# Second feed-forward matrix, block 0: one column block multiplied by halves of the rows, one with alternating PSUM banks

## The chip, the cores and the metric

The kernel runs on one core of a Trainium2 chip. The time is that of the device, in microseconds, for one execution of the whole program on that core. The engines that matter are TensorE (PE in the profile; its weight loads are listed apart as PEld), VectorE (DVE), ScalarE (ACT), GpSimd (POOL) and the queue of SyncE (SP), which issues the loads of weights. TensorE writes its products to PSUM banks of 128 partitions by 512 float32 values.

## What is computed

One encoder layer over 256 positions of width 2048: attention with a window, then a feed-forward part, each with scale, shift and gate from a conditioning vector and followed by a layer norm. The change is in the feed-forward part:

```python
def sq_relu_mlp(h, w1, b1, w2, b2):
    u = jnp.square(jax.nn.relu(h @ w1 + b1))
    return u @ w2 + b2
...
y = sq_relu_mlp(hff, mlp_w1[i], mlp_b1[i], mlp_w2[i], mlp_b2[i])
x = layer_norm(DEEPNORM_ALPHA * x + (1.0 + g_f[:, None, :]) * y, ln_mlp_g[i], ln_mlp_b[i])
```

Here `h` is 256 x 2048, `w1` is 2048 x 8192 and `w2` is 8192 x 2048, all float32.

## The kernel before

**Products.** TensorE is fed float32r, a shorter float32. So that little is lost, every operand is split into a high part (a rounded copy, made on ScalarE, line 277 for weights) and a low part (the difference, made on VectorE, line 230), and one product of 128 x 128 by 128 x 512 is three matmuls into the same bank: high by high, high by low, low by high (`mm3`, lines 544, 545 and 546). Each matmul loads its stationary operand, the activations, anew; the weights are the moving operand.

**Blocks.** The 8192 hidden columns go in four blocks of 2048 (`BLK = 4`). Block 0 first makes its hidden values `us` with lines 1032 to 1034, and then multiplies them with its 2048 rows of the second matrix. Only in block 0 is this done for all four column blocks `c` of 512 outputs in the plain way by `ff_out` and `ff_mm`; blocks 1 to 3 mix the first matrix with half of the second one (`ff_mixed`, whose first matmuls are those of line 1060) and use `ff_out` for the column blocks 2 and 3 alone.

**One column block.** `ff_out` takes two banks, one for each half `t` of the 256 positions. It goes through 16 slices `k` of 128 hidden columns: four loads of weights (`kg`), in each two pairs of slices (`k2`), in each pair first the six matmuls of `t` = 0 and then the six of `t` = 1. That is 16 x 2 x 3 = 96 matmuls. After each pair `S.done()` gives a pair of weight buffers back, and more weights are prepared. After the column block two adds on VectorE (line 1179) bring the two banks and the bias row to SBUF, one add for each `t`; with them the banks come free.

**Banks.** The pool `psa` has five banks for all of these products (`bufs=5`); two more pools hold the remaining three banks. A tile taken from the pool gets a bank that nothing uses any more; the first matmul into it waits until the last reader of the tile before is through.

**The order of work.** Each engine runs its instructions in a fixed order, which is set when the program is built: by the order in the source, except where an instruction that comes later in the source is ready sooner. `Stream` (`S`) keeps the weights in order: it loads 128 x 2048 slices on the queue of SyncE, makes high and low parts in five buffers each, and between them gives VectorE the steps of the second gate (`m_gf`, `Mod.step`, line 378), two multiply-adds of 128 x 1024 for each slice of the gate's matrix. During block 0 a number of these slices are spread among the weights by the list `gf_fill`. The adds of line 1179 stand in the same queue of VectorE as those steps and the low parts.

Elsewhere the kernel has products that use only 64 of the 128 rows of the array: the scores of the attention (line 733), in plain float32, where two heads lie on the partitions 0 to 63 and 64 to 127 and write to two banks in turn. Every such product of the source is two instructions of 64 x 128 by 64 x 256 in the trace.

Of the kernel before, what the change touches and what calls it, by code (L numbers as in the profile page):

```python
# [11 lines left out]
F32 = mybir.dt.float32  # L12
# [8 lines left out]
S = 256  # L21
NT = S // 128
# [26 lines left out]
def hybrid_kernel(ctx: ExitStack, tc: tile.TileContext, a, out: bass.AP):  # L49
    nc = tc.nc  # L50
# [7 lines left out]
    psa = ctx.enter_context(tc.tile_pool(name="psa", bufs=5, space=PSUM))  # L58
# [9 lines left out]
    def g4b(dt=F32):  # L68
        if not more:
            early.close()  # L70
            more.append(ctx.enter_context(tc.tile_pool(name="gen2", bufs=2 * MORE)))
        return more[0].tile([128, 1024], dt, tag="g4b", name="g4b")

    def g4(dt=F32):
        return gen.tile([128, 1024], dt, tag="g4", name="g4")
# [93 lines left out]
    def bias_all(src, b):  # L169

        for h in range(2):
            nc.gpsimd.dma_start(b[h], src[:, h * 1024:h * 1024 + 1024].partition_broadcast(128))
        return lambda c: b[c // 2][:, (c % 2) * 512:(c % 2) * 512 + 512]
# [139 lines left out]
    S = Stream()  # L313
# [155 lines left out]
    for g in range(2, G):  # L469
        n = len(ORDER[g])  # L470
# [69 lines left out]
    def part(tiles, t, c):  # L540
        return tiles[c][:, t * 512:t * 512 + 512]

    def mm3(ps, xh, xl, wh, wl, start, stop):
        nc.tensor.matmul(ps, xh, wh, start=start, stop=False)  # L544
        nc.tensor.matmul(ps, xh, wl, start=False, stop=False)  # L545
        S.prev = nc.tensor.matmul(ps, xl, wh, start=False, stop=stop).ins  # L546
# [62 lines left out]
    def qkv(g, ch):  # L609

        _, k0, nk = m_mix[g]
        hh, hl = held[g]
        wh, wl = S.main()
        per = 4 // nk
        for ci in range(per):
            p = ch * per + ci
            c = CORD[p]
            go_on, held_back = c in half, ((g, ch), p) in CARRY
            pss = half.pop(c, None) or banks()
            for k2 in range(0, nk, 2):  # L620
                for t in range(NT):
                    for k in (k2, k2 + 1):
                        s = slice(k * 256 + t * 128, k * 256 + t * 128 + 128)
                        mm3(pss[t], hh[:, s], hl[:, s], wh(ci * nk + k), wl(ci * nk + k),
                            k == 0 and not go_on, k == nk - 1 and not held_back)
                S.done()
                if per == 1 and k2 == 0:
                    yield
            if held_back:
                half[c] = pss  # L630
            else:
                evict(c, pss)
            if per == 2 and ci == 0:
                yield
# [36 lines left out]
    for x, (g, c) in enumerate(qk_order):  # L671
        at = ORDER[g].index(c)
        mid = []
# [156 lines left out]
    def project(j, c):  # L830
        wh, wl = S.main()
        oh, ol = oT[j]
        pss = [psa.tile([128, 512], F32, name="pa") for _ in range(NT)]
        last = j == 3 and c == 3
        for t, rs in [(0, range(4)), (1, range(4))] if last else [(t, (r, r + 1)) for r in (0, 2) for t in range(NT)]:
            for r in rs:
                s = slice(t * 512 + r * 128, t * 512 + r * 128 + 128)
                mm3(pss[t], oh[:, s], ol[:, s], wh(r), wl(r), r == 0, r == 3)
            if t == 1 or last:
                S.done(not last)  # L840
            if last:
                add_gated(pss[t], t, c, g1, st)
                sc.append(norm_scalars(st[t]))
                normed(0, t)
            if t == 1 and rs[0] == 0:
                yield
        for t, ps in enumerate(pss):
            if j == 0:
                nc.vector.tensor_add(part(ys, t, c), ps, bo(c))
            elif j < 3:  # L850
                y = part(ys, t, c)
                nc.vector.tensor_add(y, y, ps)
                if j == 2:
                    z = part(xs, t, c)
                    nc.vector.tensor_mul(y, y, g1(c))
                    nc.vector.scalar_tensor_tensor(z, z, ALPHA, y, op0=OP.mult, op1=OP.add)
            elif not last:
                add_gated(ps, t, c, g1, st)
# [11 lines left out]
    def mids(n):  # L870
        out = []
        if 0 < n <= 16:
            out.append(lambda: probs_T(n - 1))
        if n < 16:
            out.append(lambda: normalise(n))
        return out
# [3 lines left out]
    for n in range(21):  # L880
# [10 lines left out]
        if n + 1 < len(LATE):  # L891
            w = qkv(*LATE[n + 1])
        else:
            if n == 5:
                ys, bo = [g4b() for _ in range(4)], bias_all(a["bo"], [g4b(), g4b()])
            w = project((n - 5) // 4, (n - 5) % 4)
        mid = mids(n)
# [116 lines left out]
    us = []  # L1014
    opened = {}
    for n, (kg, fq) in enumerate(W1A):
# [3 lines left out]
        wh, wl = S.main()  # L1020
        for fp in range(2):
            if kg % 2 == 0:
                opened[fq, fp] = psa.tile([128, 512], F32, name="pa")
            ps = opened[fq, fp]
            for fi in range(2):
                o = ps[:, fi * 256:fi * 256 + 256]
                for k in range(4):
                    w = (fp * 2 + fi) * 4 + k
# [10 lines left out]
            elif kg == 3:  # L1039
                nc.vector.tensor_add(av, av, ps)  # L1040
                u = g4(F32R)
# [67 lines left out]
    def gather(pm):  # L1109

        y = [part(ys, t, c) for t in range(NT) for c in range(2)]
        w = sml.tile([128, 512], F32, name="w", tag="t2", bufs=4)

        def add(d, *ops):
            return lambda: nc.vector.tensor_add(d, *ops)

        return [add(y[0], y[0], pm[2]), lambda: nc.scalar.copy(w, pm[6]), add(y[1], y[1], pm[3]),
                add(y[2], y[2], pm[4]), add(y[0], y[0], pm[1]), add(w, w, pm[1]), add(y[1], y[1], w),
                add(y[1], y[1], pm[5]), add(y[3], y[3], pm[5]), add(w, w, pm[7]), add(y[2], y[2], w),
                add(y[3], y[3], w)]  # L1120

    def ff_mm(ps, us, kg, t, w, start, stop, ks=range(4)):
        wh, wl = w
        for k in ks:
            n = 4 * kg + k
            s = slice((n % 2) * 256 + t * 128, (n % 2) * 256 + t * 128 + 128)
            u = us[n // 2]
            mm3(ps, u[:, :512][:, s], u[:, 512:][:, s], wh(k), wl(k), start and k == 0, stop and k == 3)

    def ff_out(blk, us, c, mid=()):  # L1130
        mid = list(mid)
        pss = [psa.tile([128, 512], F32, name="pa") for _ in range(NT)]
        for kg in range(4):
            w = S.main()
            for k2 in (0, 2):
                for t in range(NT):
                    ff_mm(pss[t], us, kg, t, w, kg == 0, kg == 3, (k2, k2 + 1))
                S.done()
                for f in mid[:2]:
                    f()  # L1140
                del mid[:2]
        return pss

    ys = [g4b() for _ in range(4)]
# [3 lines left out]
    def rescale(c):  # L1148
        gb = [sml.tile([128, 512], F32, name="gb", tag="t2", bufs=4) for _ in range(2)]
        for n in range(2):  # L1150
            nc.gpsimd.dma_start(gb[n], a["lnrow"][n:n + 1, c * 512:c * 512 + 512].partition_broadcast(128))
        for t in range(NT):
            z = part(xs, t, c)
            nc.vector.scalar_tensor_tensor(z, z, ALPHA, gb[0], op0=OP.mult, op1=OP.mult)
            nc.vector.scalar_tensor_tensor(z, gb[1], ALPHA, z, op0=OP.mult, op1=OP.add)

    def base(c, ts=range(NT)):
        for t in ts:
            y, z = part(ys, t, c), part(xs, t, c)
            nc.vector.tensor_mul(y, y, g2(c))  # L1160
            nc.vector.tensor_add(z, z, y)

    def row_bias(c):
        b = sml.tile([128, 512], F32, name="bf", tag="t2", bufs=4)
        nc.gpsimd.dma_start(b, a["b2"][:, c * 512:c * 512 + 512].partition_broadcast(128))
        return b

    for blk in range(BLK - 1):
        if blk:
            us, pm = ff_mixed(blk)  # L1170
        for c in (2, 3) if blk else range(4):
            mid = gather(pm) if blk and c == 2 else []
            for f in mid[:2]:
                f()
            if blk == 0:
                bf = row_bias(c)
            for t, ps in enumerate(ff_out(blk, us, c, mid[2:])):
                if blk == 0:
                    nc.vector.tensor_add(part(ys, t, c), ps, bf)
                else:  # L1180
                    nc.vector.tensor_add(part(ys, t, c), part(ys, t, c), ps)
            if blk:
                rescale(2 * blk + c - 4)
        if blk == 0:
            S.reserve = 2

    blk = BLK - 1
    g2 = gate(m_gf)
    us, pm = ff_mixed(blk, [lambda c=c, t=t: base(c, (t,)) for c in (2, 3) for t in range(NT)])
# [5 lines left out]
    mid = gather(pm)  # L1195
    for f in mid[:2]:
        f()
    pss = ff_out(blk, us, 2, mid[2:])
    for c in range(2):
        base(c)  # L1200
# [7 lines left out]
    for t in range(NT):  # L1208
        ps = psa.tile([128, 512], F32, name="pa")
# [108 lines left out]
```

## Time and profile before

| | |
|---|---|
| median of the runs | 1080.25 us (2 runs, 1079.69 and 1080.81) |
| the profiled execution | 1080.82 us, of which the span from the first to the last instruction is 1079.0 us |
| mean granted TensorE clock | 0.995 of full speed |
| DMA over the span | 292.70 MB, mean 271 GB/s |

"Busy" is the time in which at least one instruction of the engine runs. The ends of matmuls are modelled, and neighbours overlap in the trace: a matmul of 128 x 512 is listed with 390 ns, but the next one starts about 227 ns after it. What such a matmul costs is therefore read from start to start. In the lists of instructions in order of time the columns are start, duration (both in us), engine, line, operation, tiles and shapes, and in brackets the idle time before it with what ended it. In the tables by stretch the columns are the stretch, its length, and for each engine the busy time and the number of instructions that started, then the granted clock, the share of the DMA engines and GB/s.

### The profile page before, as it was taken

To read this page: it belongs to the slowest core of one execution; us is meant where nothing else is said; L and a number is where in the kernel's file an instruction comes from. 1 tells how busy PE (TensorE), PEld (TensorE's weight loads), DVE (VectorE), ACT (ScalarE), POOL (GpSimd) and SP (SyncE) were. 2 spreads that over 40 slices of the span, in tenths; PEclk is the share of its full clock that TensorE was granted. 3 is DMA by queue.
4 is the path that set the end of the run, shared out by engine and by line. 5 is a ranking of instruction groups with operands and counts; after the bars stand their busy time and mean duration, and the time that the engine had idled before them with its cause. 6 is when DMAs were issued, how large, how long until landed. Compare 5 with 4: busy or idle time off the path is not lost.

```text
span 1079.0 us, 15651 instructions
## 1 busy us (share of the span) xinstructions
PE 1049.8 (97%) x6018; PEld 847.9 (79%) x6018; DVE 926.3 (86%) x1371; ACT 611.4 (57%) x977; POOL 31.0 (3%) x56
## 2 busy tenths in 40 slices
PE   8889999999999999999999999999999999999995
PEld 6557677666667799988888888888888888888884
DVE  5598699988889898988679889969988887998997
ACT  5333347776773636644357677347767536776740
POOL 1000000001000000000000000000000001000001
PEclk9999999999999999999999999999999999999998
DMA  9999997779966798689725644954464684455632
GB/s 384 425 426 426 426 419 268 283 281 378 405 251 234 305 356 314 257 335 405 271 97 196 233 176 153 375 195 176 176 234 174 266 319 148 176 205 220 244 161 78
DMA packets 43371, 292.70 MB, mean 271 GB/s; under 512 B 5136, under 2 KB 5264, under 8 KB 9504
## 3 DMA queue, kind: packets, MB, share of 16 engines
q1 hardware_dynamic: 39312, 279.85, 66.7%
q0 software_dynamic: 3232, 10.50, 3.0%
q10 hardware_dynamic: 752, 1.35, 0.3%
q8 instruction: 47, 0.77, 0.3%
q14 instruction: 28, 0.23, 0.1%
HBM read 289.57 MB, written 2.11 MB: 270 GB/s over the span
## 4 chain that ended last, share of the span: by engine, by line
PE 85%; DMA 9%; DVE 4%; ACT 1%; issue 0%; SPq 0%; DVEq 0%; ACTq 0%
PE pa L1060 17%; PE pa L544 13%; PE pa L546 13%; PE pa L545 13%; PE pa L1062 8%; DMA raw<-in_wqkv 4%; PE pa L1033 3%; PE pa L1034 3%; PE pa L1032 3%; DMA raw<-in_modm 3%; PE pm L340 2%; DMA raw<-in_modf 2%; PE pa L733 1%; PE pa L789 1%; DVE wl L230 1%; DVE g L378 1%
## 5 line engine op out<-in xcount | busy, mean ns | idle before, releaser
L277 ACT CAST wh<-raw 128x1024 fp32r<-128x1024 f32 (+1 forms) x332 | 335.5, 1020 | 302.3 <-PE pa L546 136.2
L230 DVE TENSOR_TENSOR wl<-raw,wh 128x1024 fp32r<-128x1024 f32 (+1 forms) x332 | 388.5, 1183 | 79.8 <-ACT wh L277 74.6
L544 PE MATMUL pa<-wh,g 128*128 128x512 f32 x648 | 258.0, 399 | 4.4 <-ACT g L581 2.1
L546 PE MATMUL pa<-wh,g 128*128 128x512 f32 x648 | 252.2, 392 | 3.0 <-DVE g L567 2.4
L545 PE MATMUL pa<-wl,g 128*128 128x512 f32 x648 | 254.0, 392 | 0.0
L1060 PE MATMUL pa<-g,wh 128*128 128x512 f32 x768 | 193.4, 394 | 0.0
L1060 PEld LDWEIGHTS pa<-g,wh 128*128 128x128 f32 x768 | 139.8, 188 | 31.6 <-DVE rl L990 4.1
L544 PEld LDWEIGHTS pa<-wh,g 128*128 128x128 f32 x648 | 121.6, 188 | 39.3 <-issue 6.8
L546 PEld LDWEIGHTS pa<-wh,g 128*128 128x128 f32 x648 | 121.6, 188 | 33.1 <-DVE g L567 4.7
L545 PEld LDWEIGHTS pa<-wl,g 128*128 128x128 f32 x648 | 121.8, 188 | 25.9 <-issue 2.4
L1062 PEld LDWEIGHTS pa<-g,wl 128*128 128x128 f32 x768 | 104.8, 190 | 7.5
L1062 PE MATMUL pa<-g,wl 128*128 128x256 f32 x768 | 107.1, 283 | 0.0
L378 DVE SCALAR_TENSOR_TENSOR g<-raw,cact,g 128x1024 f32<-128x1024 f32 x65 | 82.6, 1278 | 1.5 <-DMA raw<-in_modf 1.3
L1033 PE MATMUL pa<-g,wh 128*128 128x256 f32 x256 | 72.7, 285 | 0.4 <-DVE g L961 0.4
L1032 PE MATMUL pa<-g,wh 128*128 128x256 f32 x256 | 72.6, 285 | 0.0
L1034 PE MATMUL pa<-g,wl 128*128 128x256 f32 x256 | 72.5, 284 | 0.0
L230 DVE TENSOR_TENSOR raw<-raw 128x1024 fp32r<-128x1024 f32 x48 | 58.7, 1223 | 8.5 <-ACT raw L277 6.6
L277 ACT CAST raw<-raw 128x1024 fp32r<-128x1024 f32 x48 | 50.6, 1054 | 12.0 <-PE pm L546 10.7
L340 PE MATMUL pm<-raw,cact 128*32 128x256 f32 (+2 forms) x768 | 47.3, 375 | 5.6 <-DMA raw<-in_modm 4.5
L1033 PEld LDWEIGHTS pa<-g,wh 128*128 128x128 f32 x256 | 49.1, 192 | 1.3 <-DVE g L961 0.8
L1032 PEld LDWEIGHTS pa<-g,wh 128*128 128x128 f32 x256 | 49.0, 192 | 0.4 <-ACT g L953 0.4
L1034 PEld LDWEIGHTS pa<-g,wl 128*128 128x128 f32 x256 | 49.1, 192 | 0.0
(220 smaller groups left out, 1210.0 us busy)
## 6 DMA issues: line engine op xcount, KB each, us to landing
raw<-in_w1b SPq DMA_DIRECT2D x48, 1024.0 KB, 5.6
raw<-in_w SPq DMA_DIRECT2D x40, 1024.0 KB, 8.4
raw<-in_modm SPq DMA_DIRECT2D x32, 1024.0 KB, 16.0
raw<-in_modf SPq DMA_DIRECT2D x32, 1024.0 KB, 8.8
raw<-in_wqkv SPq DMA_DIRECT2D x24, 1024.0 KB, 11.8
raw<-in_w2s SPq DMA_DIRECT2D x24, 1024.0 KB, 4.8
raw<-in_modgm SPq DMA_DIRECT2D x16, 1024.0 KB, 8.4
raw<-in_wo SPq DMA_DIRECT2D x16, 1024.0 KB, 7.6
```

Of the source, the lines that this page charges most:

```text
L230: self.pinned(nc.vector.tensor_sub(l[:, :w], r, f32(self.hs[n])[:, :w]))
L277: self.pinned(nc.scalar.copy(h[:, :s.shape[-1]], s))
L340: i = nc.tensor.matmul(self.ps[32 * j:32 * j + 32, :w], lhsT[j] if type(lhsT) is list else lhsT, rhs[j], start=self.first, stop=stop)
L378: nc.vector.scalar_tensor_tensor(p[:, :e], s, cact[:, kt:kt + 1], p[:, :e], op0=OP.mult, op1=OP.add)
L544: nc.tensor.matmul(ps, xh, wh, start=start, stop=False)
L545: nc.tensor.matmul(ps, xh, wl, start=False, stop=False)
L546: S.prev = nc.tensor.matmul(ps, xl, wh, start=False, stop=stop).ins
L1032: nc.tensor.matmul(o, wh(w, 128), hh, start=new, stop=False)
L1033: nc.tensor.matmul(o, wh(w, 128), hl, start=False, stop=False)
L1034: nc.tensor.matmul(o, wl(w, 128), hh, start=False, stop=end)
L1060: nc.tensor.matmul(ps, wh(k, 128), ff_in(k), start=k == 0, stop=False)
L1062: nc.tensor.matmul(ps[:, :256], wl(k, 128), ff_in(k)[:, :256], start=False, stop=k == NK - 1)
```

## The change

The second and the third column block of block 0 are done in other ways; the first and the fourth stay as they are.

For the second one (`c` = 1), `ff_out` takes four banks, two for each `t`. Every matmul over 128 rows becomes two over 64 rows each, `halves`: rows 0 to 63 into one bank, rows 64 to 127 into the other, in turn. The column block has 192 matmuls of 64 x 128 by 64 x 512 in place of 96 of 128 x 128 by 128 x 512. Each `t` then has two adds on VectorE, the first with the bias row and the first bank, the second with the second bank: four adds in place of two.

For the third one (`c` = 2), `ff_turns` does the same 96 matmuls in another order: for each slice and each of its three products, first `t` = 0 and then `t` = 1, so that two matmuls in a row never have the same bank or the same stationary operand.

```diff
+    def halves(ps, xh, xl, wh, wl, start, stop):
+        for n, (x, w) in enumerate(((xh, wh), (xh, wl), (xl, wh))):
+            for r in range(2):
+                p = slice(64 * r, 64 * r + 64)
+                S.prev = nc.tensor.matmul(ps[r], x[p], w[p], start=start and n == 0, stop=stop and n == 2).ins
+
+    def ff_turns(pss, us, kg, w, ks):
+        wh, wl = w
+        for k in ks:
+            n = 4 * kg + k
+            u = us[n // 2]
+            for m, (x, y) in enumerate(((0, wh), (0, wl), (512, wh))):
+                for t in range(NT):
+                    s = slice(x + (n % 2) * 256 + t * 128, x + (n % 2) * 256 + t * 128 + 128)
+                    nc.tensor.matmul(pss[t], u[:, s], y(k), start=n + m == 0, stop=n == 15 and m == 2)
...
-            mm3(ps, u[:, :512][:, s], u[:, 512:][:, s], wh(k), wl(k), start and k == 0, stop and k == 3)
+            (halves if split else mm3)(ps, u[:, :512][:, s], u[:, 512:][:, s], wh(k), wl(k),
+                                       start and k == 0, stop and k == 3)
...
-        pss = [psa.tile([128, 512], F32, name="pa") for _ in range(NT)]
+        pss = [[psa.tile([128, 512], F32, name="pa") for _ in range(2)] if split else
+               psa.tile([128, 512], F32, name="pa") for _ in range(NT)]
...
-                for t in range(NT):
-                    ff_mm(pss[t], us, kg, t, w, kg == 0, kg == 3, (k2, k2 + 1))
+                if blk == 0 and c == 2:
+                    ff_turns(pss, us, kg, w, (k2, k2 + 1))
+                else:
+                    for t in range(NT):
+                        ff_mm(pss[t], us, kg, t, w, kg == 0, kg == 3, (k2, k2 + 1), split)
...
-            for t, ps in enumerate(ff_out(blk, us, c, mid[2:])):
-                if blk == 0:
+            for t, ps in enumerate(ff_out(blk, us, c, mid[2:], blk == 0 and c == 1)):
+                if blk == 0 and c == 1:
+                    nc.vector.tensor_add(part(ys, t, c), ps[0], bf)
+                    nc.vector.tensor_add(part(ys, t, c), part(ys, t, c), ps[1])
+                elif blk == 0:
                     nc.vector.tensor_add(part(ys, t, c), ps, bf)
```

More of the change, by code (lines that the diff above doesn't have):

```diff
@@ L1120, in gather, with ff_mm @@
                 add(y[3], y[3], w)]
-    def ff_mm(ps, us, kg, t, w, start, stop, ks=range(4)):
+    def halves(ps, xh, xl, wh, wl, start, stop):
[12 more added lines that the diff above has]
+                    nc.tensor.matmul(pss[t], u[:, s], y(k), start=n + m == 0, stop=n == 15 and m == 2)
+    def ff_mm(ps, us, kg, t, w, start, stop, ks=range(4), split=False):
         wh, wl = w
@@ L1127, in ff_mm, with ff_out @@
             u = us[n // 2]
-            mm3(ps, u[:, :512][:, s], u[:, 512:][:, s], wh(k), wl(k), start and k == 0, stop and k == 3)
-    def ff_out(blk, us, c, mid=()):
+            (halves if split else mm3)(ps, u[:, :512][:, s], u[:, 512:][:, s], wh(k), wl(k),
+                                       start and k == 0, stop and k == 3)
+    def ff_out(blk, us, c, mid=(), split=False):
         mid = list(mid)
-        pss = [psa.tile([128, 512], F32, name="pa") for _ in range(NT)]
+        pss = [[psa.tile([128, 512], F32, name="pa") for _ in range(2)] if split else
+               psa.tile([128, 512], F32, name="pa") for _ in range(NT)]
         for kg in range(4):
```

## The prediction

> **What bounds the kernel now.** I first read the page: the span, the busy shares and the chain of waits.
>
> ```profile
> span 1079.0 us, 15651 instructions
> PE 1049.8 (97%) x6018; PEld 847.9 (79%) x6018; DVE 926.3 (86%) x1371; ACT 611.4 (57%) x977; POOL 31.0 (3%) x56
> ...
> PE 85%; DMA 9%; DVE 4%; ACT 1%; issue 0%; SPq 0%; DVEq 0%; ACTq 0%
> ```
>
> TensorE is busy in 97% of the span and carries 85% of the chain that ended last. Time added to TensorE's stream comes out at the end unless a later wait shrinks, and there is hardly a later wait. Next I read the table by stretch where the change lies.
>
> ```profile
> 480.00:490.00 10.00, 10.00 (x46) 8.29 (x45) 10.00 (x10) 2.14 (x3) 0.00 (x0) 1.00 0.88 340
> 490.00:500.00 10.00, 10.00 (x46) 8.29 (x45) 10.00 (x11) 5.49 (x6) 0.00 (x0) 1.00 1.00 422
> 510.00:520.00 10.00, 10.00 (x46) 8.29 (x45) 6.99 (x6) 4.05 (x4) 0.00 (x0) 1.00 0.74 258
> ```
>
> TensorE has no gap here, at full clock. But from 480 to 500 VectorE too is busy in every microsecond: it has a backlog, and whoever comes to need VectorE there has to queue. Which column block this is, I get from the matmuls of line 1060 that follow block 0, and from the list of TensorE's instructions in order of time.
>
> ```profile
> L1060 PE MATMUL pa<-g,wh x768: 387/390/505, 547.7 to 1014.0; 128*128 128x512 f32 x192
> ```
> ```profile
> 480.62 0.39 PE L545 MATMUL pa<-wl,g 128*128 128x512 f32 x1
> 480.84 0.39 PE L546 MATMUL pa<-wh,g 128*128 128x512 f32 x1
> 481.07 0.39 PE L544 MATMUL pa<-wh,g 128*128 128x512 f32 x1
> ...
> 482.20 0.39 PE L546 MATMUL pa<-wh,g 128*128 128x512 f32 x1
> 482.43 0.39 PE L544 MATMUL pa<-wh,g 128*128 128x512 f32 x1
> ...
> 484.24 0.39 PE L546 MATMUL pa<-wh,g 128*128 128x512 f32 x1
> ...
> 503.96 0.39 PE L546 MATMUL pa<-wh,g 128*128 128x512 f32 x1
> ```
>
> From 480.62 to 484.24 there are 16 steps, so a matmul costs 0.2263 us from start to start; from 482.43 to 503.96 there are 95, 0.2266 each. I take 0.2266. Counting three blocks of 96 back from 547.7 gives 547.7 - 288 x 0.2266 = 482.4: the row at 482.43 is the first matmul of the second column block, 503.96 its last. The first column block had ended its matmuls for t = 0 just ahead of 481.07 (six before 482.43) and those for t = 1 just ahead of 482.43. Now VectorE's list.
>
> ```profile
> 477.58 1.28 DVE L378 SCALAR_TENSOR_TENSOR g4b<-raw,cact,g4b 128x1024 f32<-128x1024 f32 x1 [2.72 <-DMA raw<-in_modgf]
> ...
> 482.25 4.87 DVE L378 SCALAR_TENSOR_TENSOR g4b<-raw,cact,g4b 128x1024 f32<-128x1024 f32 x4
> 487.04 1.22 DVE L230 TENSOR_TENSOR wl<-raw,wh 128x1024 fp32r<-128x1024 f32 x1
> 488.17 2.48 DVE L378 SCALAR_TENSOR_TENSOR g4b<-raw,cact,g4b 128x1024 f32<-128x1024 f32 x2
> 490.56 1.28 DVE L1179 TENSOR_TENSOR g4b<-pa,bf 128x512 f32<-128x512 f32 x2
> 491.76 2.35 DVE L230 TENSOR_TENSOR wl<-raw,wh 128x1024 fp32r<-128x1024 f32 x2
> ...
> 502.75 1.23 DVE L230 TENSOR_TENSOR wl<-raw,wh 128x1024 fp32r<-128x1024 f32 x1 [0.57 <-ACT wh L277]
> 503.90 1.28 DVE L1179 TENSOR_TENSOR g4b<-pa,bf 128x512 f32<-128x512 f32 x2
> ```
>
> The two adds that empty the first column block's banks run at 490.56, 8 us after its last matmul, behind six gate steps and a low part. Today nobody waits for them: the second column block takes two of the three other banks of the five. The second column block's own adds run at 503.90, promptly.
>
> **The change part by part.**
>
> *The banks, the main term.* The second column block now wants four banks, and five less the first block's two leaves three. The fourth, for t = 1 and the upper rows, has to wait for the first of the adds at 490.56.
>
> ```profile
> L1179 DVE TENSOR_TENSOR g4b<-pa,bf x8: 680/683/685, 490.6 to 548.0; 128x512 f32<-128x512 f32 x8
> ```
>
> With 0.68 us for the add the bank is free at 491.24. What stands ahead of the add on VectorE comes before the second column block in the source, so it needs none of its matmuls and the stall doesn't delay it. TensorE reaches the blocked product early: six pairs of t = 0, then one half for t = 1, then the blocked half. How long a pair takes I read from the scores, the only products on halves of the rows.
>
> ```profile
> 218.63 0.39 PE L546 MATMUL pa<-wh,g 128*128 128x512 f32 x1
> 218.95 1.14 PE L733 MATMUL pa<-g,g 64*128 64x256 f32 x8
> 220.01 0.50 PE L544 MATMUL pa<-wh,g 128*128 128x512 f32 x1
> 220.35 0.40 PE L545 MATMUL pa<-wl,g 128*128 128x512 f32 x1
> ```
>
> In the stretch 219.44 to 219.47 the same list shows the pair that is under way:
>
> ```profile
> 219.27 0.38 PE L733 MATMUL pa<-g,g 64*128 64x256 f32 x2
> ```
>
> Two matmuls lie in 0.38 us, the duration of one: they do run at once. The eight are four pairs. The second starts at 219.27, 0.32 after the first; the last at 218.95 + 1.14 - 0.38 = 219.71, two steps of 0.22 further. A plain float32 half of 256 columns isn't a float32r half of 512. Bounds for the new pair: 0.22 (as these) and 0.453 (one after the other, each like a full matmul). I take 0.22, the row that is nearest in shape, and keep the other end as a rival. The blocked half is then due at 482.43 + 0.09 (the switch, below) + 0.32 + 5 x 0.22 = 483.94. Stall: 491.24 - 483.94 = **+7.3 us**. If VectorE's queue is one low part (1.22) or one gate pair (2.48) shorter or longer, it moves by as much. Behind the blocked half, all of TensorE's stream is queued; ScalarE and VectorE meanwhile fill their five buffers and stop, which gains nothing in a stage where TensorE had no gaps.
>
> *The clock.* A stall of this length has a price of its own. Here is the longest idle stretch of TensorE early on, in its list and in the table by stretch.
>
> ```profile
> 25.38 0.50 PE L544 MATMUL pa<-wh,g 128*128 128x512 f32 x1 [2.12 <-ACT g L581]
> ```
> ```profile
> 23.30:25.40 2.10, 0.02 (x1) 0.02 (x1) 2.01 (x3) 2.10 (x4) 0.00 (x0) 1.00 1.02 433
> 26.60:30.00 3.40, 3.40 (x57) 2.46 (x53) 0.00 (x0) 1.26 (x3) 0.00 (x0) 0.50 1.02 429
> 30.00:31.00 1.00, 0.59 (x21) 0.32 (x17) 0.00 (x0) 0.00 (x0) 0.00 (x0) 1.00 0.98 401
> 48.00:52.00 4.00, 1.94 (x26) 0.85 (x22) 4.00 (x8) 1.05 (x1) 0.00 (x0) 1.00 1.01 424
> ```
>
> After 2.1 us of idling the granted clock was 0.50 for 3.4 us, though TensorE was busy again; another gap of 2.06 us (48 to 52) cost nothing. 7.3 us is well above both. Price: half of 3.4, **+1.7 us**; bounds 0 (the slow stretch falls inside the stall) and 3.4 (two of them). The Trainium skill ("TensorE: Matmul & The Clock Gate", Part 1) says that an idle window of about 3.4 us halves the clock and that a whole busy one restores it, with windows that run freely; by that rule the slow clock is certain here, and an estimate of the loss is 1.7 to 3.4 us. The trace agrees in the length of the slow stretch.
>
> *The switches.* Into halves: 218.63 to 218.95 is 0.32 where 0.23 is usual, +0.09; first to second pair 0.32 where 0.22 follows, +0.10. Back: 219.71 to 220.01, 0.30, +0.08; then 0.34 to the next, +0.11. Once each: **+0.4 us**.
>
> *The pairs.* 96 pairs at 0.22 in place of 96 matmuls at 0.2266: **-0.6 us**. The rule that speaks against this is in the Trainium skill ("TensorEngine Tiling (Array Packing)", Instruction Overhead): about 60 cycles of overhead for each matmul on this chip. For the 96 added ones an estimate by that rule at 2.4 GHz is 96 x 25 ns = +2.4 us. The trace doesn't bear it out: a pair costs less than one full matmul.
>
> *The adds.* Two more of 0.68 us on VectorE, which idles 3.0 of 10 us in 510 to 520; they sit on no path of their own. But of the five banks only one is then free, the first block's second; the third column block needs, for its second matmul, the bank that the first of these adds empties: due at 503.96 + 0.30 + 0.23 = 504.49 in the old times, free at 503.90 + 0.68 = 504.58. **+0.1 us**; up to 1.3 if a low part (1.22) is ahead of it, 0 if VectorE is early.
>
> *The third column block.* The banks change today after every six matmuls, at 481.07 and 482.43: 0.23 from the row before both times, like the steps without a change. So **0**. Bounds: -0.6 (if alternating banks gave the 0.22 of the pairs) and +1.0 (0.01, what the rows' rounding hides, on 96). Weights are ready for whole pairs of slices, so the other order of high and low waits for nothing new. No load, cast or DMA is moved.
>
> *Sum.* 7.3 + 1.7 + 0.4 - 0.6 + 0.1 + 0 = **+8.9 us**. The profiled execution took 1080.8 (1.8 more than its span); with the sum 1089.7. It lies 0.6 above the median of the runs, so I forecast **1089** for a median. With the bounds of the stall, the clock and the pairs: 1086 to 1093.
>
> **The rivals.**
>
> *Filled stall.* When the program is built, products of the lower rows and of t = 0 may be put ahead of the blocked ones. For: low parts of weights are made while the adds still wait (487.04), so there is work to put ahead. Against: in 480 to 484 the lines run in strict source order. A group of t = 0 (6 x 0.22 = 1.3) and one of unpaired lower halves (1.3) fill 2.6 each, and each unpaired group costs 1.3 later. Three of them fill the stall and keep the clock: 3 x 1.3 + 0.4 - 0.6 + 0.1 = +3.8, 1084.
>
> *No stall, not slower.* The adds of the first column block could come forward to its end, ahead of the four gate steps at 482.25. The bank for t = 0 is then free before 483.9, and what is left is 0.4 - 0.6 + 0.1: 1080. It decides if the adds run before about 483.2. Against: they stand behind steps that precede them in the source, and nothing in the change moves them.
>
> *Not two at once.* If float32r halves run one after the other, 96 x (0.453 - 0.2266) = +21.7; the blocked half is due later, at 482.5 + 12 x 0.2266 + 0.23 = 485.5, so the stall is 5.8; with 1.7, 0.4 and 0.1 it is +29.7, 1110. For: the float32 halves take 0.22 for 256 columns, so each delivers a column only half as fast as a float32r half would, and no row shows two banks written at the full rate. Against: two banks are separate targets, and the pairs in the trace do overlap. A weaker form, every pair at 0.32 like the first, gives 96 x 0.093 = +9.0 with a stall of 6.8: 6.8 + 1.7 + 0.4 + 9.0 + 0.1 = +18, 1098.
>
> **How the numbers follow.** Chances: stall as summed 0.56, filled 0.18, no stall 0.10, pairs at 0.32 0.03, one after the other 0.12, a gain by something unseen 0.01. The range 1080 to 1098 takes in the first four, and the bounds of the unknown prices; the serial case is left out. About 2% (21.6 us) is what a measurement of this kernel can tell from no change: 1102 is passed only by the serial case and tails of the weaker one, 0.13; nothing gives 2% of gain, since all that the two column blocks could save is under 2 us, 0.01; within, 0.86.
>
> **What would show it.** A gap on TensorE of about 7 us some 1.5 us after the second column block begins, ended by VectorE's line of the bias add, and granted clock 0.50 right behind it; no gap means the no-stall rival, a gap split up by lone halves the filled one. Pairs of 64 x 128 matmuls that begin within some 10 ns, 0.22 from pair to pair: right; 0.45: serial. In the third column block 0.2266 from start to start. I am wrong if the sum of these differs, or if the stage after 548 grows or shrinks.

## The result, and the profile after

The changed kernel takes 1095.35 us (median of 2 runs, 1095.33 and 1095.37), against 1080.25 before: 1.014 times as long, 95% interval 1.0096 to 1.0183. That is +15.1 us between the medians and +14.55 between the two profiled executions (1095.37 and 1080.82); the forecast was +8.9. The time lies inside the predicted range of 1080 to 1098, 6 us above the predicted one, and above the 1086 to 1093 that the bounds of the summed terms gave.

The page of the changed kernel: span, busy time by engine, shares of the chain that ended last.

```profile
span 1093.6 us, 15846 instructions
...
PE 1058.0 (97%) x6114; PEld 852.5 (78%) x6114; DVE 927.1 (85%) x1373; ACT 611.0 (56%) x977; POOL 31.0 (3%) x56
...
PE 79%; DVE 10%; DMA 7%; ACT 2%; issue 2%; DVEq 0%; ACTq 0%; SPq 0%
```

TensorE is busy for 8.2 us longer, though the change adds no products; part of it are matmuls at a lower clock and halves that ran alone, as shown below. And 6 points of the chain have gone over from TensorE to VectorE. (There are 96 more matmuls, and two more instructions of VectorE, which are the two new adds.)

The tables by stretch, one row for a column block, from its first matmul to the next one's; columns as in the prediction. Before, the second and the third column block:

```profile
482.43:504.19 21.76, 21.76 (x98) 18.02 (x96) 21.19 (x20) 8.12 (x8) 0.00 (x0) 1.00 0.97 399
504.19:525.95 21.76, 21.76 (x98) 18.02 (x96) 15.70 (x15) 8.44 (x8) 0.00 (x0) 1.00 0.88 336
```

After, the second, the third and the fourth:

```profile
483.27:512.75 29.48, 25.29 (x193) 20.55 (x192) 20.73 (x19) 8.40 (x8) 0.00 (x0) 0.94 0.88 344
512.75:539.48 26.73, 23.76 (x98) 19.27 (x98) 17.35 (x18) 8.43 (x8) 0.00 (x0) 0.94 0.62 236
539.48:561.23 21.75, 21.75 (x97) 18.02 (x96) 11.26 (x11) 8.44 (x8) 0.00 (x0) 1.00 0.56 193
```

The second block is longer by 7.72 us, the third by 4.97, the fourth by nothing. Both of the long ones hold idle time of TensorE (29.48 - 25.29 = 4.19, and 26.73 - 23.76 = 2.97) and a clock of 0.94. What is left of the 14.6 lies outside: 0.84 ahead of the second block (which starts at 483.27, not 482.43) and 1.06 behind the fourth.

TensorE's list of the changed kernel, around the two gaps; each gap is in brackets with what ended it.

```profile
482.95 0.39 PE L546 MATMUL pa<-wh,g 128*128 128x512 f32 x1
483.27 0.50 PE L1126 MATMUL pa<-wh,g 64*128 64x512 f32 x2
...
487.28 0.39 PE L1126 MATMUL pa<-wh,g 64*128 64x512 f32 x1
491.86 0.50 PE L1126 MATMUL pa<-wh,g 64*128 64x512 f32 x1 [4.20 <-DVE g4b L1203]
...
501.56 0.62 PE L1126 MATMUL pa<-wh,g 64*128 64x512 f32 x4
502.01 0.40 PE L1126 MATMUL pa<-wl,g 64*128 64x512 f32 x2
502.24 0.63 PE L1126 MATMUL pa<-wh,g 64*128 64x512 f32 x4
...
512.75 0.50 PE L1136 MATMUL pa<-wh,g 128*128 128x512 f32 x1
516.22 0.73 PE L1136 MATMUL pa<-wh,g 128*128 128x512 f32 x1 [2.97 <-DVE g4b L1200]
```

The same kernel's table by stretch, right behind each gap:

```profile
492.43:495.84 3.41, 3.41 (x17) 2.61 (x16) 3.41 (x3) 1.04 (x1) 0.00 (x0) 0.50 1.02 428
516.32:519.73 3.41, 3.41 (x8) 2.64 (x9) 3.06 (x4) 0.00 (x0) 0.00 (x0) 0.50 0.98 399
```

The first gap was forecast in place and cause: the blocked half of t = 1 waits for VectorE's bias add of the first block (line 1203, before at 1179). Of the second only the waiter was forecast, at 0.1 us: the second matmul of the third block waits for the adds of the second block (line 1200), and these came late. Behind each gap the granted clock is 0.50 for 3.41 us, which costs 1.7. The Trainium skill ("TensorE: Matmul & The Clock Gate", Part 1) has an idle window of about 3.4 us halve the clock; the trace agrees in the length of the slow stretch, while the second gap was only 2.97 us long. The last section comes back to which gaps slow the clock.

From 501.56 to 502.24 six halves start (four with high, two with low weights), then the next six in the same pattern: 3 pairs in 0.68 us, 0.227 for a pair. That is what a full matmul costs, not 0.22.

VectorE's list of the changed kernel, around both sets of adds (lines 1203, then 1200 and 1201):

```profile
488.73 2.48 DVE L378 SCALAR_TENSOR_TENSOR g4b<-raw,cact,g4b 128x1024 f32<-128x1024 f32 x2
491.12 1.28 DVE L1203 TENSOR_TENSOR g4b<-pa,bf 128x512 f32<-128x512 f32 x2
...
511.95 2.48 DVE L378 SCALAR_TENSOR_TENSOR g4b<-raw,cact,g4b 128x1024 f32<-128x1024 f32 x2 [2.22 <-DMA raw<-in_modgf]
514.35 1.22 DVE L230 TENSOR_TENSOR wl<-raw,wh 128x1024 fp32r<-128x1024 f32 x1
515.48 0.68 DVE L1200 TENSOR_TENSOR g4b<-pa,bf 128x512 f32<-128x512 f32 x1
```

Here is the cause of the second gap. VectorE stood still for 2.22 us for a slice of the gate's matrix, then did the pair of gate steps and a low part, and only then the adds at 515.48, 2.7 us after the second block's last matmul. In the kernel before, the adds ran at 503.90, while such a gate step came 8 us later:

```profile
510.92 1.22 DVE L230 TENSOR_TENSOR wl<-raw,wh 128x1024 fp32r<-128x1024 f32 x1 [1.49 <-ACT wh L277]
512.06 1.28 DVE L378 SCALAR_TENSOR_TENSOR g4b<-raw,cact,g4b 128x1024 f32<-128x1024 f32 x1
```

The order of VectorE's instructions, fixed when the program is built, is another one. Around the second block's adds it was: low part, two adds, three low parts, gate step. It is now: two gate steps, low part, four adds, low part, gate steps. In the source the gate steps still come after the adds and five low parts; the fifth experiment, which holds them to it, shows that order.

### The profile page after: what moved, and what is told of

Its sections match the earlier page's. It is cut to its first block, busy times and chain, and to the rows that moved or that the text cites. A ratio compares the mean times of both kernels' runs of the same rounds, so it can differ in the third digit from the quotient of the medians.

```text
span 1093.6 us, 15846 instructions
## 1 busy us (share of the span) xinstructions
PE 1058.0 (97%) x6114; PEld 852.5 (78%) x6114; DVE 927.1 (85%) x1373; ACT 611.0 (56%) x977; POOL 31.0 (3%) x56
## 4 chain that ended last, share of the span: by engine, by line
PE 79%; DVE 10%; DMA 7%; ACT 2%; issue 2%; DVEq 0%; ACTq 0%; SPq 0%
PE pa L1060 15%; PE pa L544 11%; PE pa L546 11%; PE pa L545 11%; PE pa L1062 7%; DVE wl L230 3%; PE pm L340 3%; PE pa L1033 2%; PE pa L1034 2%; DMA raw<-in_wqkv 2%; PE pa L1032 2%; PE pa L1136 2%; DMA raw<-in_modm 2%; PE pa L733 2%; PE pa L789 1%
## 5 line engine op out<-in xcount | busy, mean ns | idle before, releaser
L544 PE MATMUL pa<-wh,g 128*128 128x512 f32 x584 | 233.8, 401 | 4.5 <-ACT g L581 2.2
L546 PE MATMUL pa<-wh,g 128*128 128x512 f32 x584 | 227.8, 394 | 2.4 <-DVE g L567 2.4
L545 PE MATMUL pa<-wl,g 128*128 128x512 f32 x584 | 229.7, 393 | 0.0
L544 PEld LDWEIGHTS pa<-wh,g 128*128 128x128 f32 x584 | 110.0, 188 | 37.4 <-issue 6.3
L546 PEld LDWEIGHTS pa<-wh,g 128*128 128x128 f32 x584 | 110.4, 189 | 29.8 <-DVE g L567 4.4
L545 PEld LDWEIGHTS pa<-wl,g 128*128 128x128 f32 x584 | 110.3, 189 | 23.6 <-issue 2.4
```

## Experiments

My theory after the result: two separate losses. The second block lacks a bank until VectorE's queue has come to the first block's adds (gap, slow clock, lone halves); the third block waits for adds that were put behind a late gate step. The alternation costs nothing, and halves in pairs cost what full matmuls cost. Rivals: that the alternation makes the second loss; that halves are slow by themselves. The times by column block below are taken from the first matmul of a block to the first of the next, for the blocks 2, 3 and 4; before they are 21.76, 21.76, 21.76. "Beside" is the median of the kernel before on the same chip. The edits shift the lines of the adds by up to 3: those of the first block stand at 1201 to 1206, those of the second at 1198 to 1204, and the text says which are meant.

**The alternation alone.** The second block as before, the third in turns.

```diff
-            for t, ps in enumerate(ff_out(blk, us, c, mid[2:], blk == 0 and c == 1)):
-                if blk == 0 and c == 1:
+            for t, ps in enumerate(ff_out(blk, us, c, mid[2:], False)):
+                if False:
```

> The third column block in turns, the second one as before. Theory (a switch of banks or of the stationary operand costs nothing, and the third block's loss in the changed kernel is its wait for a bank): third block 21.8 us as before, total within 1 us of the kernel before. Rival (the order in turns is itself what made the third block 26.7 us): third block about 26 us, total about 5 us above the kernel before.

Measured: 1081.83 beside 1081.36, ratio 1.0005 (0.9992 to 1.0017); blocks 21.76, 21.76, 21.76. Alternating banks cost nothing and save nothing.

**The halves alone.** The third block as before.

```diff
-                if blk == 0 and c == 2:
+                if False:
```

> The second column block in halves, the third one as before. Theory (a wait for banks twice): second block 29.5 us as in the changed kernel; in the third block the first matmul for t = 1 comes 6 matmuls late instead of 1, so of the 3.2 us of waiting some 2 us are left, with up to 1.7 us for the clock: total 9.5 to 13 us above the kernel before. Rival (the turns cost the 5 us of the third block): third block 21.8 us, total 8 us above.

Measured: 1094.96, ratio 1.0126 (1.0105 to 1.0146); blocks 29.65, 25.59, 21.76. The second loss is there without the alternation, so it comes from the halves: a gap ended by line 1200, with the clock at 0.50 behind it from 515.37 on for 3.4 us.

```profile
515.23 0.69 PE L544 MATMUL pa<-wh,g 128*128 128x512 f32 x1 [1.79 <-DVE g4b L1200]
```

The halves alone make +13.6, a little above the 13 that I had expected at most.

**The halves with banks to spare.** For the upper rows the two banks of the pool `pst` are taken, which are not in use in this stage. The alternation stays off.

```diff
-        pss = [[psa.tile([128, 512], F32, name="pa") for _ in range(2)] if split else
+        pss = [[psa.tile([128, 512], F32, name="pa"), pst.tile([128, 512], F32, name="pt")] if split else
```

> As the halves alone, but the two added banks come from the pool of the transposes, which is idle here; so no bank is short. Theory: no gap on TensorE, clock 1.00, second block 21.8 + 0.4 us for the switches with pairs at 0.227, total within 1 us of the kernel before. Rival (halves are slow by themselves, or halve the clock): second block above 27 us, total at least 5 us above.

Measured: 1089.01, ratio 1.0073 (1.0053 to 1.0092); blocks 22.01, 27.67, 21.76. The second block has no gap: the first loss is a matter of banks, and in this count the halves cost 0.25 us more than full matmuls, a part of the switch into them and out of them. But I missed the total: the third block is 5.9 us longer, though now no bank can be short in it. In its VectorE list:

```profile
508.19 2.48 DVE L378 SCALAR_TENSOR_TENSOR g4b<-raw,cact,g4b 128x1024 f32<-128x1024 f32 x2 [6.94 <-DMA raw<-in_modgf]
510.59 1.22 DVE L230 TENSOR_TENSOR wl<-raw,wh 128x1024 fp32r<-128x1024 f32 x1
511.73 0.68 DVE L1200 TENSOR_TENSOR g4b<-pa,bf 128x512 f32<-128x512 f32 x1
```

and in TensorE's list of the same run:

```profile
515.79 0.50 PE L545 MATMUL pa<-wl,g 128*128 128x512 f32 x1 [0.79 <-DVE wl L230]
...
521.76 0.80 PE L545 MATMUL pa<-wl,g 128*128 128x512 f32 x1 [2.95 <-DVE wl L230]
```

VectorE stands still for 6.94 us in front of a gate step whose slice hasn't landed, with low parts queued behind it; TensorE then waits for low parts, 0.79 and 2.95, and has one slow stretch of clock. The same misplaced gate step as in the changed kernel shows in another waiter.

**Four banks with whole rows.** 96 full matmuls as before, but for each t the products with high weights go into one bank and those with low weights into a second one, so that four banks and four adds are needed without halves. The alternation stays off here too.

```diff
-            for r in range(2):
-                p = slice(64 * r, 64 * r + 64)
-                S.prev = nc.tensor.matmul(ps[r], x[p], w[p], start=start and n == 0, stop=stop and n == 2).ins
+            S.prev = nc.tensor.matmul(ps[n % 2], x, w, start=start and n < 2, stop=stop and n > 0).ins
```

> No halves: the 96 matmuls of the second column block keep all 128 rows, but for each t the products go by turns to two banks of the same pool, so that four are taken and four adds made. Theory (the want of a bank is the whole cost): second block 27 to 30 us, with a gap that ends at the first block's first add, and again some loss in the third block; total 8 to 13 us above the kernel before. Rival (the halves are the cost): total within 1 us of the kernel before.

Measured: 1084.45, ratio 1.0026 (1.0014 to 1.0038); blocks 23.81, 21.76, 21.76. I missed: a gap of the same length was expected. TensorE's list:

```profile
490.55 1.20 PE L1124 MATMUL pa<-wl,g 128*128 128x512 f32 x4 [1.75 <-DVE g4b L1201]
```

The blocked group waits here too, for the first block's add (line 1201). But the time ahead of it was filled at full rate with 30 matmuls: the products of t = 0, and for t = 1 those whose bank was free (four of every six). So 1.75 us are left, and the clock stayed at 1.00. And the third block lost nothing: VectorE's order is the one of before, in spite of four adds and four banks. So it is the halves, or the doubled number of matmuls that comes with them, that change the order. Why the build orders VectorE differently beside 192 short matmuls (perhaps it reckons the block longer, and so the slice in time) was not tested.

**Spare banks, and the gate steps held in their place.** The third experiment, with the gate steps held to the order of the source from the second column block on (`S.late` is set ahead of each block).

```diff
-                            nc.vector.scalar_tensor_tensor(p[:, :e], s, cact[:, kt:kt + 1], p[:, :e],
-                                                           op0=OP.mult, op1=OP.add)
+                            i2 = nc.vector.scalar_tensor_tensor(p[:, :e], s, cact[:, kt:kt + 1], p[:, :e],
+                                                                op0=OP.mult, op1=OP.add)
+                            if S.late:
+                                tc.keep_in_program_order(i2)
...
+            S.late = blk == 0 and c > 0
```

> Halves with spare banks, third block as before, and the gate steps from the second block on may not be put ahead of VectorE instructions that precede them in the source. Theory (with enough banks the 5.9 us that the third block lost came from a gate step that was put ahead of the adds and low parts and waited 6.9 us for its load): second block 22.0 us, third block 21.8 us, no gap, total 0.3 to 2 us above the kernel before. Rival (the weights come late for another reason): third block about 27 us again, total 7 us above.

Measured: 1082.15 beside 1081.06, ratio 1.0013 (1.0001 to 1.0024); blocks 22.01, 21.91, 21.76. Both gaps are gone; the 0.15 that the third block keeps is the end of the switch out of halves. VectorE's list:

```profile
502.17 1.23 DVE L230 TENSOR_TENSOR wl<-raw,wh 128x1024 fp32r<-128x1024 f32 x1 [0.81 <-ACT wh L277]
503.31 0.68 DVE L1203 TENSOR_TENSOR g4b<-pa,bf 128x512 f32<-128x512 f32 x1
...
517.16 2.48 DVE L378 SCALAR_TENSOR_TENSOR g4b<-raw,cact,g4b 128x1024 f32<-128x1024 f32 x2
```

The second block's adds (line 1203 here) follow a low part, and the gate steps come 14 us later without an idle VectorE ahead of them.

**The change with the gate steps held.** The same edit in the changed kernel: no spare banks, alternation on.

> The changed kernel, five banks and turns, with the gate steps held behind what precedes them in the source. Theory (two separate losses): second block about 29.5 us as in the changed kernel, third block 22 to 23.5 us with a short wait for the first add and no slow clock; total 8 to 10 us above the kernel before, the sum of the prediction. Rival (the third block's wait for its bank is long in any order): third block 26 us, total 14 us above.

Measured: 1089.89, ratio 1.0090 (1.0075 to 1.0105), +8.8 us; blocks 29.38, 22.03, 21.76. TensorE's list, and the adds of the second block in VectorE's:

```profile
491.80 0.58 PE L1128 MATMUL pa<-wh,g 64*128 64x512 f32 x1 [4.12 <-DVE g4b L1206]
...
512.36 0.39 PE L1128 MATMUL pa<-wh,g 64*128 64x512 f32 x1
512.67 0.86 PE L1138 MATMUL pa<-wh,g 128*128 128x512 f32 x2
```
```profile
512.29 0.68 DVE L1203 TENSOR_TENSOR g4b<-pa,bf 128x512 f32<-128x512 f32 x1
```

The first loss stays whole (line 1206 is the first block's add), the second is gone: the second block's adds run at 512.29, and the third block starts without a gap. The two losses are separate: spare banks take away the first one alone, the held order the second one alone.

**The gate steps later.** To empty VectorE's queue ahead of the first block's adds, gate slices are moved from the early entries of `gf_fill` to later ones in the changed kernel.

```diff
-    gf_fill = [3, 0, 1, 0, 0, 1, 4, 1, 0, 0, 0, 0, 0, 1, 1, 0, 0, 0, 1, 0, 0, 0, 0, 1, 0, 0, 0, 1, 0, 1, 0, 0]
+    gf_fill = [3, 0, 1, 0, 0, 0, 0, 0, 0, 0, 0, 0, 0, 0, 0, 0, 1, 1, 1, 1, 0, 1, 1, 1, 1, 1, 1, 1, 0, 1, 0, 0]
```

> The changed kernel with five banks and turns, but the gate's slices that were spread over the second to the fourth column block and the blocks after it are all planned after block 0, so VectorE has no queue when the first block's banks are full. Theory (the want of a bank costs only as long as VectorE's queue is): no gap in the second block, 22.0 to 22.5 us; third block 21.8 to 22.5 us; total 0 to 3 us above the kernel before, with the later stages carrying the moved steps. Rival (four banks of five are too few whatever VectorE does): second block above 25 us, total at least 5 us above.

Measured: 1092.21, ratio 1.0113 (1.0097 to 1.0129); blocks 22.00, 22.02, 21.76, then 543.5 us to the end in place of 531.3. VectorE's list has the adds promptly:

```profile
483.37 1.28 DVE L1203 TENSOR_TENSOR g4b<-pa,bf 128x512 f32<-128x512 f32 x2
```

With the adds at 483.37 in place of 491.12 the change costs next to nothing in its own blocks, with five banks. The want of a bank costs just what VectorE's queue makes of it. No gate step stands near the second block's adds either, so the second loss is gone too. The total was missed, because the stretch behind block 0 grew by 12.2 us (in the profiled execution, which took 1094.85). VectorE is busy there for 488.2 us in place of 470.3, and TensorE, which had no waits there before, has 7.4 us of them; what makes the rest was not traced. The two largest waits (total us, times, longest):

```profile
PE pa L545 <- DVE wl L230: 3.2, 4, 1.5
PE pa L544 <- ACT wh L277: 3.0, 2, 1.7
```

**Halves issued apart.** Are the pairs made by issuing lower and upper rows in turn? First the fifth experiment with the loops exchanged: three lower halves, then three upper.

```diff
-        for n, (x, w) in enumerate(((xh, wh), (xh, wl), (xl, wh))):
-            for r in range(2):
+        for r in range(2):
+            for n, (x, w) in enumerate(((xh, wh), (xh, wl), (xl, wh))):
```

> As the halves with spare banks and held gate steps, but in each slice first the three products on the lower rows, then the three on the upper rows. Theory (two matmuls run at once only where neighbours in the stream have different rows; here that is 1 of 3): 4 steps for 6 matmuls, second block 29.3 us, total 7.5 to 10 us above the kernel before. If nothing overlaps: 43.8 us, total 22 us above. If the order of the halves doesn't matter: 22.0 us, total 0.3 to 2 us above.

Measured: 1081.79 beside 1081.06, ratio 1.0016 (1.0006 to 1.0025); blocks 22.01, 21.92, 21.76. My theory missed: it had two halves at once only where neighbours in the stream have different rows, which would have made the second block 29.3 us. What came true is the third case, that the order doesn't matter. TensorE's list, with `pa` for lower rows and `pt` for upper:

```profile
489.72 0.39 PE L1128 MATMUL pa<-wh,g 64*128 64x512 f32 x1
489.73 0.39 PE L1128 MATMUL pt<-wh,g 64*128 64x512 f32 x1
489.94 0.39 PE L1128 MATMUL pa<-wh,g 64*128 64x512 f32 x1
489.95 0.39 PE L1128 MATMUL pt<-wh,g 64*128 64x512 f32 x1
490.17 0.39 PE L1128 MATMUL pa<-wl,g 64*128 64x512 f32 x1
490.18 0.39 PE L1128 MATMUL pt<-wl,g 64*128 64x512 f32 x1
490.40 0.39 PE L1128 MATMUL pa<-wh,g 64*128 64x512 f32 x1
```

Lower and upper start 0.01 us apart, though in the source three of a kind stand together. Then runs of 12 and 12, as in the diff, and of 24 and 24, with the loop over the rows put outside the one over the pairs of slices:

```diff
+                    for r in range(2):
+                        for t in range(NT):
+                            ff_mm(pss[t], us, kg, t, w, kg == 0, kg == 3, (k2, k2 + 1), True, [(r,)])
```

> Halves with spare banks and held gate steps, in stretches of 12: for each pair of slices first the 12 products on the lower rows of both t, then the 12 on the upper rows. Theory A (lower and upper halves are taken from the program some way ahead, each as soon as its own rows are free, as the run with stretches of 3 suggests): second block 22 to 23 us. Theory B (the order of the program is kept, and the overlap with stretches of 3 came from neighbours): 1 of 12 overlaps, second block about 41 us.

> As the run before it, in stretches of 24 (one load of weights). Theory A: 22 to 23 us if the look ahead reaches 24 matmuls with their weight loads; if it reaches only part of that, between 23 and 42 us. Theory B: 1 of 24 overlaps, about 42 us.

Measured, one run each: 1091.03 and 1098.76 beside 1082.3; second block 32.30 and 38.51, third 21.91 in both. Neither theory gave these numbers: in pairs it would be 22.0, one after the other 192 x 0.2267 + 0.25 = 43.8. Without the 0.25 for the switch, one of the 8 stretches of 24 halves takes 4.0 us, 17.7 steps of 0.2267, and one of the 4 stretches of 48 takes 9.57, 42.2 steps. Each stretch has two changes from one row group to the other, so in both kernels about three steps are saved at each. The end of a lower run in the 12 and 12 kernel shows how:

```profile
483.62 0.39 PE L1128 MATMUL pa<-wl,g 64*128 64x512 f32 x1
483.85 0.39 PE L1128 MATMUL pa<-wh,g 64*128 64x512 f32 x1
483.85 0.49 PE L1128 MATMUL pt<-wh,g 64*128 64x512 f32 x1
484.08 0.39 PE L1128 MATMUL pa<-wh,g 64*128 64x512 f32 x1
484.19 0.39 PE L1128 MATMUL pt<-wl,g 64*128 64x512 f32 x1
...
484.54 0.39 PE L1128 MATMUL pa<-wh,g 64*128 64x512 f32 x1
484.65 0.39 PE L1128 MATMUL pt<-wh,g 64*128 64x512 f32 x1
484.88 0.39 PE L1128 MATMUL pt<-wl,g 64*128 64x512 f32 x1
```

The upper rows begin at 483.85, beside the ninth of the twelve lower halves; the twelfth starts only at 484.54.

**The whole change with spare banks and order held.** The fifth experiment with the alternation on.

> The whole change, halves and turns, with spare banks and held gate steps. Theory (want of banks and the moved gate step are the whole loss; halves and turns neither gain nor cost more than the switches): second block 22.2 us, third block 21.8 us, total 0.3 to 2 us above the kernel before. Rival (halves and turns together cost something that neither does alone): third block above 23 us.

Measured: 1081.27 beside 1082.3, ratio 0.9998 (0.9987 to 1.0008); blocks 22.01, 21.91, 21.76. Without its two waits the change is worth nothing either way. No version beat the kernel before.

## Why the prediction came out as it did

The +14.6 of the profiled execution, by place: 0.84 ahead of the second block, 7.72 in it, 4.97 in the third, 1.06 behind the fourth.

*Stall, forecast +7.3: right in place, cause and waiter; 2.7 of it was filled.* The blocked half was due at 483.94 by the prediction, 484.78 with the later start of 0.84. TensorE first did six pairs, six lone lower halves of t = 1, six pairs of t = 0 of the next slices, and then stood until 491.86. Start to start the gap is 491.86 - 487.28 - 0.23 = 4.35. The two groups put ahead filled 2 x 1.36 = 2.7, and the add came 0.3 early on that scale: 7.3 - 2.7 - 0.3 = 4.3. So one step of the "filled stall" rival did happen; what the prediction held against it, that the lines run in strict source order, was wrong for this point. The six upper halves that were left without a partner cost 6 x 0.227 = 1.36 later. Gap and lone halves make 5.7 of the forecast 7.3.

*Clock, +1.7: right* for the second block, one stretch of 3.41 us at 0.50.

*Switches, +0.4: about right,* 0.49 in the experiments with spare banks and held order: 0.25 in the second block (22.01 against 21.76), 0.15 in the third (21.91), and 0.09 ahead of the second, where the first half starts 0.32 after the last full matmul (482.95 to 483.27 in the changed kernel) in place of 0.23. With the 0.25 the second block is accounted for: 4.35 + 1.36 + 1.7 + 0.25 = 7.66 of 7.72.

*Pairs, -0.6:* 0. A float32r pair of 512 columns takes 0.227 like a full matmul, not the 0.22 of the float32 pairs. The rivals with slow pairs fell. Nor do the runs bear out the overhead for each matmul (the Trainium skill, "TensorEngine Tiling (Array Packing)", Instruction Overhead), by which the prediction gave +2.4: 96 more matmuls in 22.01 us leave 0.25 for everything.

*Alternation, 0: right* (the first experiment).

*Adds, +0.1 with a bound of 1.3: this is the step that failed.* The prediction named the right wait, the third block's second matmul for the second block's adds, and priced it from the VectorE order of before: the adds at once, or at most one low part later. The change moved a gate pair ahead of them, and this pair waits for its load. The gap is 516.22 - 512.75 - 0.23 = 3.24 us and brings a slow stretch of its own, 1.7: 4.9 of the 4.97. The prediction took VectorE's order as unmoved ("No load, cast or DMA is moved"); that is true of the source and false of the built order. That the order did it is shown: held, with nothing else changed, the third block takes 22.03, and the whole kernel takes +8.8 us.

Even this agrees with the forecast of +8.9 only because errors cancel: the stall with its lone halves is 1.6 less than forecast, the pairs 0.6 more and the switches 0.1 more, which makes 8.0, and the other 0.8 lies outside the two blocks.

*The range: held by luck.* The summed terms with their bounds gave 1086 to 1093. What carried the range on to 1098 was the rival with every pair at 0.32, and a pair took 0.227. The loss that brought the time to 1095 had been bounded at 1.3 and cost 4.9. By the prediction's own sign, a sum of gap, clock and pairs that differs, its account was incomplete.

*The rival without a stall* named its condition rightly: adds ahead of about 483.2. With the gate steps moved away they ran at 483.37 and the second block took 22.00.

*The 0.84 ahead of the second block.* Of this 0.09 is the switch into halves. The other 0.75 goes with something far ahead of the change: in the changed kernel's trace the clock is 0.50 from 120.37 us on for 3.41 us, and in the trace of before it is not. The five profiled executions with such a stretch near 120 us begin the second block at 483.27 to 483.76, the eight without one at 481.52 to 482.76. So it is a difference between executions, and I don't count it to the change.

Left open: the 1.06 behind the fourth block. In the other profiled executions that stretch is up to 1.8 us longer than before, without a pattern (the experiment with moved gate steps aside), and in the last experiment it is 1.05 longer although the median is that of before. I give it no cause.

## What to carry to other kernels

Where a change needs more accumulators, look not at when their last matmul ends but at when the emptying engine's queue comes to them: five banks sufficed with a prompt VectorE and cost 7.7 us with one that had 8 us of work ahead. Where the build chooses the order of an engine, an edit on TensorE can reorder VectorE, so bound each handover by what stands near it in the queue, waits for loads included, and not by its present place; the instruction that waits for a DMA is the one to look for. And splitting products that already fill the array buys nothing, since two halves at once cost as much as the whole.

## What the runs showed of the hardware

Halves on different rows overlap without being issued in turn: 3 and 3 in the program ran as full pairs (22.01 us), and at the change from one row group to the other about three steps overlap whether the runs are 12 long or 24. The Trainium skill ("TensorE: Matmul & The Clock Gate", Part 3) has matmuls start strictly in the order of the program, with only weight loads taken ahead; these runs differ from that, unless the build or a step after it reorders them; the runs can't tell these apart.

Gaps of 4.2 and of 2.97 us each brought exactly one stretch of 3.41 us at clock 0.50; one of 1.75 us brought none. A wait of 3 us thus cost 4.9.

Length alone doesn't decide. The gap of 1.79 us with the halves alone did slow the clock, and in the kernel before one of 2.12 us did (the one ended at 25.38) while one of 2.06 us didn't (the one ended at 51.61). What fits all of these is where the gap lies. Slow stretches of one trace begin whole multiples of 3.413 us apart (492.43 and 516.32: 7 of them), so one can lay windows of this length over a trace. The gaps of 4.2, 2.97, 2.12 and 1.79 left more than half of one window idle (2.85, 2.97, 2.12 and 1.79 of its 3.41 us), and the next window ran at 0.50. The gaps of 2.06 and 1.75 were cut by a border (0.93 and 1.13; 1.23 and 0.52) and cost no clock. A sharp bound doesn't come out: in the thirteen traces windows with 1.4 to 1.9 us of idling went both ways, those with more all brought a slow one. So the 1.7 us that such a gap adds depends in part on where it falls.
